# Attention values in a two-layer decoder trunk: unmasked weights on the left chunk's v, masked weights on the difference of both chunks' v, 512 columns a matmul

## The chip, the cores and the metric

The kernel runs on one core of one Trainium2 chip. The metric is the device time of one execution in microseconds (us). Before the change it is 2219.04 us, the median of three runs (2216.8 to 2220.34). The engines are called TensorE (PE, and PEld for its weight loads), VectorE (DVE), ScalarE (ACT), GpSimd (POOL) and SyncE (SP).

## The reference, cut to what matters

Input x is 2048 tokens by 1024 features, in float32. A first layer (a gated MLP with a spatial mix inside chunks of 128 tokens) is followed by a second: attention in a sliding window of 128 tokens, with 16 query heads of 64 features, 2 key/value heads, and a sink per head in the softmax. A query of chunk n sees keys of its own chunk and of the chunk to its left:

```python
k_band, v_band = band(k), band(v)          # chunk to the left, own chunk
rel = kj - CHUNK - qi
in_window = (rel <= 0) & (rel > -WINDOW)   # exactly 128 keys for each query
scores = where(mask, q . k_band * HEAD_DIM ** -0.5, -inf)
m = maximum(max(scores), sink)
p = exp(scores - m)
p = p / (sum(p) + exp(sink - m))
o = einsum('bnhrqk,bnkhd->bnqhrd', p, v_band)
y = o * silu(g)
return y @ w_out
```

For query i of a chunk, key j of the own chunk counts where j <= i, and key j of the left chunk where j > i. So each of the 128 places j belongs to exactly one of the two chunks, and one row of 128 weights holds them all. The trunk ends with a residual sum and a norm.

## The kernel before, in words

A float32 operand is split in two parts, high and low (`split`, L117 to L119: ACT casts the high part, DVE subtracts it from the operand). A product is then three matmuls (`mm3`, L121 to L124). The first layer (stage A) takes the first 1412 us and isn't touched. The second layer (stage B) goes through four blocks of 512 tokens, some 196 us each from the second on. A block has 18 pieces (`PIECES`): two for k and v (`kv_piece`, L879), eight for q, eight for the gate, and then the output projection (`outproj_b`, L1038). A counter of half pieces (`half`) sets off the attention steps among these matmuls: 16 tiles a block, one for four query heads and one chunk of 128 tokens, started at the counts in `ATT`. The steps of one tile are these:

- `scores` (L948): eight matmuls into two banks of PSUM (L966, L967), DVE merges the two chunks' scores into one row of 128 (L973) and takes the maximum (L974 to L982), ACT takes the exponentials (L984), and POOL divides by the sum (L991). A bank is free when ACT has read it.
- `turn_p` (L994), four half pieces later: four transposes on PE (L997), the high part on ACT (L999), the low part on DVE (L1000), then four selects on POOL (L1005): high and low with the own chunk's triangle kept, and high and low with the left chunk's triangle kept.
- `values` (L1011), three half pieces later: eight matmuls of 256 columns (L1019). The weights are v's high and low part, side by side (128 columns), so that the product has the high part's sum in one half of the partitions and the low part's in the other. The order is changed for the odd heads (low, high), for which `vst` holds the high part twice. ACT copies one half to the other's partitions (L1024, L1025), and DVE adds (L1026, L1027).

When the four tiles of a quad (four heads) are done, `gated` (L1029) multiplies by the gate (L1032) and splits for the output projection. The last quad's result is used by the fourth weight tile of the output projection, of which the first three run meanwhile. At about that time `hn_steps` (L310) also prepares the next block's input on DVE (L323, L119) and ACT (L118). POOL's queue also issues the loads of the projection weights (L190), each of which waits until PE has let go of the buffer. All short-lived tiles of stage B come from one pool of 39 slots of 512 columns (`GEN_B`). A scheduler places the instructions on each engine's queue, which is then worked off in order.

The diff touches `kv_piece`, `turn_p`, `values` and the tiles made ahead of them.

Of the kernel before, what the change touches and what calls it, by code (L numbers as in the profile page):

```python
# [12 lines left out]
F32 = mybir.dt.float32  # L13
F32R = mybir.dt.float32r
I32 = mybir.dt.int32
AF = mybir.ActivationFunctionType
ALU = mybir.AluOpType

P = 128
# [9 lines left out]
HD = 64  # L29
RING = 6  # L30
# [6 lines left out]
W_BUFS = 4  # L37
LOOKAHEAD = 3
GEN_A = 18
GEN_B = 39  # L40
RAW_A = 12
ST0 = 1
FIRST_W = (0, 2, 5)
# [19 lines left out]
def trunk(ctx: ExitStack, tc: tile.TileContext, xT, wv, wug, wao, wkv, wqg, wbo, wsT, bs, gains, lngb,  # L63
          bq, bkv, sinks, rot, masks, out):
    nc = tc.nc
    V, A, G, PE = nc.vector, nc.scalar, nc.gpsimd, nc.tensor
# [24 lines left out]
    def slot(dt=F32):  # L91
        return gen[0].tile([P, TB], dt, name="s", tag="s")

    def bank():
        return psum.tile([P, 512], F32, name="ps", tag="ps")
# [46 lines left out]
    def after(n, fn):  # L142
        at(now[0] + n, fn)
# [696 lines left out]
    bc = ctx.enter_context(tc.tile_pool(name="bc", bufs=1))  # L840
# [8 lines left out]
    sink_sb = bc.tile([P, 16], F32, name="sink_sb")  # L849
    nc.sync.dma_start(sink_sb, sinks.partition_broadcast(P))  # L850
    kst = bc.tile([P, 2, 2, RING, P], F32R, name="kst")
    vst = bc.tile([P, RING, 2, 3, HD], F32R, name="vst")
    V.memset(kst[:, :, :, RING - 1, :].bitcast(F32), 0.0)
    V.memset(vst[:, RING - 1].bitcast(F32), 0.0)

    def rope(src, nh, t0, nt, tab):
# [22 lines left out]
    def kv_piece(b, tp, w2, hh, hl, tab):  # L879
        if not w2:  # L880
            w2.extend([weights(), weights()])
        ps = bank()
        for t2 in range(2):
            natural(ps, t2, 2 * tp + t2, w2, hh, hl)
        kvs = slot()
        kv3 = kvs.rearrange("p (t n) -> p t n", t=2)
        V.tensor_tensor(kv3, ps.rearrange("p (t n) -> p t n", t=2), bkv_sb[:, None, :].broadcast_to([P, 2, 256]),
                        ALU.add)
        c0 = b * TT + 2 * tp
        kr = rope(kv3[:, :, 0:P].rearrange("p t (h d) -> p t h d", h=2), 2, 2 * tp, 2, tab)  # L890
        kr = kr.rearrange("p (t h d) -> p t h d", t=2, h=2)
        kss = []
        for t2 in range(2):
            sl = (c0 + t2) % RING
            ks = slot(F32R).rearrange("p (h s r d) -> p h s r d", h=2, s=2, r=2)
            src = kr[:, t2, :, None, :].broadcast_to([P, 2, 2, HD])
            A.copy(ks[:, :, 0], src)
            V.tensor_tensor(ks[:, :, 1], src, ks[:, :, 0].bitcast(F32), ALU.subtract)
            kss.append(ks)
            vsrc = kv3[:, t2, P:2 * P].rearrange("p (h d) -> p h d", h=2)  # L900
            A.copy(vst[:, sl, :, 0, :], vsrc)
            A.copy(vst[:, sl, :, 2, :], vsrc)
            V.tensor_tensor(vst[:, sl, :, 1, :], vsrc, vst[:, sl, :, 0, :].bitcast(F32), ALU.subtract)

        def turn():
            for t2 in range(2):
                sl = (c0 + t2) % RING
                pst = bank().bitcast(F32R)
                for i in range(4):
                    PE.transpose(pst[:, i * P:(i + 1) * P], kss[t2][:, i // 2, i % 2].rearrange("p r d -> p (r d)"),  # L910
                                 ident_r)
                A.copy(kst[:, :, :, sl, :], pst.bitcast(F32).rearrange("p (h s k) -> p h s k", h=2, s=2))

        after(K_T, turn)
# [79 lines left out]
    def turn_p(pn):  # L994
        ps = bank()
        for i in range(4):
            PE.transpose(ps[:, i * P:(i + 1) * P], pn[:, i * P:(i + 1) * P], ident)  # L997
        h_, l_ = slot(), slot()
        A.activation(h_.bitcast(F32R), ps, AF.Copy)  # L999
        V.tensor_tensor(l_, ps, h_, ALU.subtract)  # L1000
        pT = []
        for sign, base in ((1, 0), (-1, -1)):
            for x in (h_, l_):
                y = slot(F32R)
                G.affine_select(out=y.rearrange("p (h q) -> p h q", h=4), in_=x.rearrange("p (h q) -> p h q", h=4),  # L1005
                                pattern=[[0, 4], [sign, P]], base=base, channel_multiplier=-sign,
                                compare_op=ALU.is_ge, fill=0.0)
                pT.append(y)
        return [pT[:2], pT[2:]]

    def values(q, t, pT, halves, o):  # L1011
        kv = q // 2
        po = bank()
        for par in range(2):
            n = 0
            for ck in range(2):
                w = vst[:, halves[ck], kv, par:par + 2, :].rearrange("p r d -> p (r d)")
                for x in pT[ck]:
                    PE.matmul(po[:, par * 256:(par + 1) * 256], w, x[:, par * 256:(par + 1) * 256],  # L1019
                              start=n == 0, stop=n == 3)  # L1020
                    n += 1
        ov = o[:, :, t * P:(t + 1) * P]
        pe, pod = (po[:, i * 256:(i + 1) * 256].rearrange("p (i q) -> p i q", i=2) for i in range(2))
        A.copy(ov[0:64], pe[64:128])  # L1024
        A.copy(ov[64:128], pod[0:64])  # L1025
        V.tensor_tensor(ov[0:64], pe[0:64], ov[0:64], ALU.add)  # L1026
        V.tensor_tensor(ov[64:128], pod[64:128], ov[64:128], ALU.add)  # L1027
# [228 lines left out]
```

## Time and profile before

| what | value |
|---|---|
| median of three runs | 2219.04 us |
| profiled execution | 2223.57 us |
| its span | 2221.8 us |
| TensorE clock granted in it | 0.983 |
| PE busy | 2133.6 us, 96% |
| DVE busy | 1687.7 us, 76% |
| ACT busy | 1089.2 us, 49% |
| POOL busy | 1065.4 us, 48% |
| L1005, the selects on POOL | 256, 185.3 us |

The times of the profile count from the start of the span. Matmuls are pipelined: a row's duration for one matmul is its latency, and the pace is the step from one start to the next. In a row of the timeline stand the start, the duration, the engine, the line, the operation, the tiles written and read, the shapes and the count, and in brackets the idle time of the engine before it and what ended that.

### The profile page before, as it was taken

Reading aid. Unit: us, or ns where it says so; the run is one execution under the profiler, and the core shown is the slowest. Engines: PE = TensorE matmul, PEld = TensorE weight load, DVE = VectorE, ACT = ScalarE, POOL = GpSimd, SP = SyncE. Lnnn points to the kernel's source line nnn. Section 1 sums busy time; section 2 is a strip of 40 time slices with the busy share of each in tenths; the row PEclk is TensorE's granted clock in tenths of the full one; section 3 lists DMA queues with packets and bytes.
Section 4 is the critical chain, followed back from the end, with each engine's and each line's share of the span. In section 5 each row is a group of like instructions: output and inputs, shape, how many; then the busy total and the mean of one; then the engine's idle time right before and its main releaser. Section 6 shows DMA issues by size and latency. Waiting matters only on the chain.

```text
span 2221.8 us, 33592 instructions
## 1 busy us (share of the span) xinstructions
PE 2133.6 (96%) x11196; PEld 1809.7 (81%) x11196; DVE 1687.7 (76%) x2693; ACT 1089.2 (49%) x2431; POOL 1065.4 (48%) x1178
## 2 busy tenths in 40 slices
PE   7799999999899999999999899999999999999997
PEld 5578888888688777788888688898899889889986
DVE  9976778888986865766657987578867967986785
ACT  5225654445444534545444543257535834663573
POOL 3781446767544566644544445334415613451460
PEclk8899999999999999999999999999999999999999
DMA  8997555667786799634435796542463354346322
GB/s 290 318 348 243 169 183 182 197 209 242 265 297 224 265 326 330 211 117 147 154 110 157 250 324 206 197 141 102 140 225 114 127 195 163 114 128 243 115 96 95
DMA packets 208940, 441.95 MB, mean 199 GB/s; under 512 B 22656, under 2 KB 61824, under 8 KB 199552
## 3 DMA queue, kind: packets, MB, share of 16 engines
q1 hardware_dynamic: 163488, 255.76, 35.6%
q0 software_dynamic: 40672, 175.66, 21.7%
q10 hardware_dynamic: 4608, 8.39, 1.0%
q8 instruction: 89, 1.46, 0.3%
q14 instruction: 83, 0.68, 0.1%
HBM read 322.81 MB, written 116.92 MB: 198 GB/s over the span
## 4 chain that ended last, share of the span: by engine, by line
PE 45%; DVE 8%; issue 3%; ACT 2%; DMA 2%; POOL 1%; SPq 0%; DVEq 0%; POOLq 0%; ACTq 0%
PE ps L122 7%; PE ps L124 6%; PE ps L123 6%; PE ps L130 6%; PE ps L129 6%; PE ps L128 6%; PE ps L1019 2%; PE ps L997 1%; PE ps L635 1%; PE ps L966 1%; PE ps L967 1%; PE ps L938 1%; DVE hn L119 1%; DVE o L1027 1%; DVE wa L119 1%
## 5 line engine op out<-in xcount | busy, mean ns | idle before, releaser
L119 DVE TENSOR_TENSOR wa<-w_raw,wa 128x512 fp32r<-128x512 f32 x456 | 465.2, 1029 | 156.4 <-ACT wa L118 153.2
L130 PE MATMUL ps<-xh,wa 128*128 128x512 f32 x1344 | 529.5, 394 | 17.7 <-DVE wa L119 17.7
L128 PE MATMUL ps<-xh,wa 128*128 128x512 f32 x1344 | 530.9, 395 | 1.3 <-ACT s L549 1.0
L129 PE MATMUL ps<-xl,wa 128*128 128x512 f32 x1344 | 527.9, 393 | 0.0
L118 ACT CAST wa<-w_raw 128x512 fp32r<-128x512 f32 x456 | 280.5, 618 | 405.8 <-PE ps L130 303.7
L130 PEld LDWEIGHTS ps<-xh,wa 128*128 128x128 f32 x1344 | 253.2, 188 | 78.7 <-DVE wa L119 22.4
L128 PEld LDWEIGHTS ps<-xh,wa 128*128 128x128 f32 x1344 | 253.5, 189 | 57.1 <-ACT s L549 1.4
L129 PEld LDWEIGHTS ps<-xl,wa 128*128 128x128 f32 x1344 | 253.4, 189 | 55.6
L1005 POOL TENSOR_SCALAR_AFFINE_SELECT s<-s 128x512 fp32r<-128x512 f32 x256 | 185.3, 752 | 101.8 <-ACT s L999 69.5
L122 PE MATMUL ps<-w,hn 128*128 128x256 f32 x640 | 184.2, 288 | 0.0
L223 POOL TENSOR_TENSOR w_raw<-w_raw 128x512 f32<-128x512 f32 x48 | 75.0, 1565 | 226.0 <-DMA w_raw<-in_wug 134.3
L123 PE MATMUL ps<-w,hn 128*128 128x256 f32 x640 | 182.3, 285 | 0.0
L124 PE MATMUL ps<-w,hn 128*128 128x256 f32 x640 | 182.2, 285 | 0.0
L119 DVE TENSOR_TENSOR xl<-s,xh 128x512 fp32r<-128x512 f32 x168 | 137.4, 853 | 15.0 <-ACT xh L118 14.5
L190 POOL DMA_DIRECT2D w<-wb x72 | 40.6, 565 | 208.3 <-PE ps L124 182.6
L631 ACT ACTIVATE vp<-vp,nb,rs 128x128 f32<-128x128 f32 x256 | 106.7, 485 | 56.6 <-DMA vp<-v 47.8
L991 POOL TENSOR_TENSOR s<-s,rd 128x512 f32<-128x512 f32 x64 | 69.6, 1090 | 115.1 <-ACT s L999 47.0
L123 PEld LDWEIGHTS ps<-w,hn 128*128 128x128 f32 x640 | 124.0, 194 | 0.5
L122 PEld LDWEIGHTS ps<-w,hn 128*128 128x128 f32 x640 | 124.0, 194 | 0.5
L124 PEld LDWEIGHTS ps<-w,hn 128*128 128x128 f32 x640 | 123.9, 194 | 0.0
L123 PE MATMUL ps<-wa,xh 128*128 128x512 f32 x256 | 104.7, 409 | 19.0 <-DVE wa L119 18.9
L225 POOL TENSOR_TENSOR w_raw<-w_raw 128x512 f32<-128x512 f32 x48 | 66.3, 1386 | 103.2 <-DVE wa L119 102.2
(190 smaller groups left out, 5011.4 us busy)
## 6 DMA issues: line engine op xcount, KB each, us to landing
w<-wb POOLq DMA_DIRECT2D x72, 1024.0 KB, 5.3
w_raw<-in_wug SPq DMA_DIRECT2D x160, 256.0 KB, 3.3
w_raw<-in_wv SPq DMA_DIRECT2D x88, 256.0 KB, 5.4
s<-in_xT SPq DMA_DIRECT2D x80, 256.0 KB, 4.8
w_raw<-in_wao SPq DMA_DIRECT2D x80, 256.0 KB, 4.1
wb<-s POOLq DMA_DIRECT2D x72, 256.0 KB, 5.8
vp<-v SPq DMA_DIRECT2D x32, 512.0 KB, 4.6
Y_s<-s POOLq DMA_DIRECT2D x64, 256.0 KB, 3.9
```

The source lines that it names most:

```text
L118: A.copy(hi, src)
L119: (lo_eng or V).tensor_tensor(lo, src, hi.bitcast(F32), ALU.subtract)
L122: PE.matmul(ps, ah, bh, start=first, stop=False)
L123: PE.matmul(ps, ah, bl, start=False, stop=False)
L124: PE.matmul(ps, al, bh, start=False, stop=last)
L128: PE.matmul(ps, ah, bh, start=first, stop=False, skip_group_check=True)
L129: PE.matmul(ps, ah, bl, start=False, stop=False, skip_group_check=True)
L130: PE.matmul(ps, al, bh, start=False, stop=True, skip_group_check=True)
L223: G.tensor_tensor(u["22"], u["21"], u["22"], ALU.add)
L631: A.activation(v[:, c, :], v[:, c, :], AF.Identity, bias=nb[:, c:c + 1], scale=rs[:, c:c + 1])
L991: G.tensor_tensor(p4, p4, rd[:, :, None].broadcast_to([P, 4, P]), ALU.mult)
L1005: G.affine_select(out=y.rearrange("p (h q) -> p h q", h=4), in_=x.rearrange("p (h q) -> p h q", h=4), pattern=[[0, 4], [sign, P]], base=ba ...
```

## The change

For each query the weights stand in one row of 128. Where `pm` is the row with only the own chunk's triangle kept, the sum over both chunks is p times the left chunk's v plus `pm` times (own v minus left v). The new kernel computes this. `kv_piece` forms the difference of each chunk's v and its left neighbour's (`vd`; the last chunk of a piece is kept in `vl` for the next) and splits it into `vdt`. `turn_p` masks the high and the low part once, not twice. `values` does four matmuls of 512 columns, two with the unmasked parts and two with the masked ones. The pool of slots has 38 and not 39.

```diff
-GEN_B = 39
+GEN_B = 38
...
-    vst = bc.tile([P, RING, 2, 3, HD], F32R, name="vst")
+    vst = bc.tile([P, RING, 2, 2, HD], F32R, name="vst")
+    vdt = bc.tile([P, RING, 2, 2, HD], F32R, name="vdt")
+    vl = bc.tile([P, P], F32, name="vl")
+    V.memset(vl, 0.0)
...
+        vd = slot()[:, :256].rearrange("p (t n) -> p t n", t=2)
+        V.tensor_tensor(vd[:, 0], kv3[:, 0, P:2 * P], vl, ALU.subtract)
+        V.tensor_tensor(vd[:, 1], kv3[:, 1, P:2 * P], kv3[:, 0, P:2 * P], ALU.subtract)
+        A.copy(vl, kv3[:, 1, P:2 * P])
...
             A.copy(vst[:, sl, :, 0, :], vsrc)
-            A.copy(vst[:, sl, :, 2, :], vsrc)
             V.tensor_tensor(vst[:, sl, :, 1, :], vsrc, vst[:, sl, :, 0, :].bitcast(F32), ALU.subtract)
+            dsrc = vd[:, t2].rearrange("p (h d) -> p h d", h=2)
+            A.copy(vdt[:, sl, :, 0, :], dsrc)
+            V.tensor_tensor(vdt[:, sl, :, 1, :], dsrc, vdt[:, sl, :, 0, :].bitcast(F32), ALU.subtract)
...
-        for sign, base in ((1, 0), (-1, -1)):
-            for x in (h_, l_):
-                y = slot(F32R)
-                G.affine_select(out=y.rearrange("p (h q) -> p h q", h=4), in_=x.rearrange("p (h q) -> p h q", h=4),
-                                pattern=[[0, 4], [sign, P]], base=base, channel_multiplier=-sign,
-                                compare_op=ALU.is_ge, fill=0.0)
-                pT.append(y)
+        pT = [h_, l_]
+        for x in (h_, l_):
+            y = slot(F32R)
+            G.affine_select(out=y.rearrange("p (h q) -> p h q", h=4),
+                            in_=x.bitcast(F32).rearrange("p (h q) -> p h q", h=4), pattern=[[0, 4], [1, P]], base=0,
+                            channel_multiplier=-1, compare_op=ALU.is_ge, fill=0.0)
+            pT.append(y)
...
-        for par in range(2):
-            n = 0
-            for ck in range(2):
-                w = vst[:, halves[ck], kv, par:par + 2, :].rearrange("p r d -> p (r d)")
-                for x in pT[ck]:
-                    PE.matmul(po[:, par * 256:(par + 1) * 256], w, x[:, par * 256:(par + 1) * 256],
-                              start=n == 0, stop=n == 3)
-                    n += 1
+        n = 0
+        for v, pair in ((vst[:, prv, kv], pT[0]), (vdt[:, cur, kv], pT[1])):
+            w = v.rearrange("p r d -> p (r d)")
+            for x in pair:
+                PE.matmul(po, w, x, start=n == 0, stop=n == 3)
+                n += 1
```

The scheduler orders the instructions anew. Lines from L854 on have other numbers in the changed kernel (L1005 is L1013, L991 is L1000, L1019 is L1029, L984 is L993, L986 is L995, L1024 and L1025 are L1033 and L1034). Three places follow, of the kernel before and then of the changed one.

On DVE, at the start of stage B, where the first piece of k and v is taken in (L887), rotated (L863 to L867), and split for k (L898) and v (L903). Before:

```order
L887 TENSOR_TENSOR s<-ps,bkv_sb 128x512
L903 TENSOR_TENSOR vst<-s,vst 128x2x64
L863 TENSOR_TENSOR s<-s 128x256
L864 TENSOR_TENSOR s<-s 128x256
L903 TENSOR_TENSOR vst<-s,vst 128x2x64
L866 TENSOR_TENSOR s<-s 128x4x32
L867 TENSOR_TENSOR s<-s 128x4x32
L255 TENSOR_TENSOR s<-ps,ident 128x512
L898 TENSOR_TENSOR s<-s 128x2x128 x2
```

The same place in the changed kernel, where L896 and L897 are the two differences and L912 is the low part of `vdt`:

```order
L890 TENSOR_TENSOR s<-ps,bkv_sb 128x512
L909 TENSOR_TENSOR vst<-s,vst 128x2x64 x2
L866 TENSOR_TENSOR s<-s 128x256
L867 TENSOR_TENSOR s<-s 128x256
L896 TENSOR_TENSOR s<-s,vl 128x128
L869 TENSOR_TENSOR s<-s 128x4x32
L870 TENSOR_TENSOR s<-s 128x4x32
L897 TENSOR_TENSOR s<-s 128x128
L912 TENSOR_TENSOR vdt<-s,vdt 128x2x64
L255 TENSOR_TENSOR s<-ps,ident 128x512
L905 TENSOR_TENSOR s<-s 128x2x128 x2
L912 TENSOR_TENSOR vdt<-s,vdt 128x2x64
```

Three of the four added instructions now stand ahead of the split of k (L898, now L905), and one behind it.

On POOL, some 85 us into the second block, where w is the buffer of the projection weights. Before:

```order
L190 DMA w<-wb_224 128x2048
L1005 AFFINE_SELECT s<-s 128x512 x4
L190 DMA w<-wb_225 128x2048
L991 TENSOR_TENSOR s<-s,rd 128x512 x2
L1005 AFFINE_SELECT s<-s 128x512 x2
L991 TENSOR_TENSOR s<-s,rd 128x512
```

In the changed kernel:

```order
L190 DMA w<-wb_224 128x2048
L1013 AFFINE_SELECT s<-s 128x512 x2
L1000 TENSOR_TENSOR s<-s,rd 128x512
L190 DMA w<-wb_225 128x2048
L1000 TENSOR_TENSOR s<-s,rd 128x512 x2
L1013 AFFINE_SELECT s<-s 128x512 x2
```

One division by the sum (L991, now L1000) has moved from behind the weight load to ahead of it.

On ACT, at the same time, where the copies of a tile's values and the exponentials of two later tiles meet. Before:

```order
L986 ACTIVATE es<-es 128x4
L1024 COPY o<-ps 64x2x128
L1025 COPY o<-ps 64x2x128
L984 ACTIVATE s,den<-ps,nm 128x128 x8
L986 ACTIVATE es<-es 128x4
L946 COPY sg<-ps 128x512
```

In the changed kernel:

```order
L995 ACTIVATE es<-es 128x4
L993 ACTIVATE s,den<-ps,nm 128x128 x8
L995 ACTIVATE es<-es 128x4
L1033 COPY o<-ps 64x2x128
L1034 COPY o<-ps 64x2x128
L955 COPY sg<-ps 128x512
```

The two copies have moved behind the eight exponentials.

More of the change, by code (lines that the diff above doesn't have):

```diff
@@ L997, in turn_p @@
             PE.transpose(ps[:, i * P:(i + 1) * P], pn[:, i * P:(i + 1) * P], ident)
[L998 to L1001, printed above, removed]
-        for sign, base in ((1, 0), (-1, -1)):
-            for x in (h_, l_):
-                y = slot(F32R)
-                G.affine_select(out=y.rearrange("p (h q) -> p h q", h=4), in_=x.rearrange("p (h q) -> p h q", h=4),
-                                pattern=[[0, 4], [sign, P]], base=base, channel_multiplier=-sign,
-                                compare_op=ALU.is_ge, fill=0.0)
-                pT.append(y)
+        h_, l_ = slot(F32R), slot(F32R)
+        A.activation(h_, ps, AF.Copy)
+        V.tensor_tensor(l_, ps, h_.bitcast(F32), ALU.subtract)
+        pT = [h_, l_]
[5 more added lines that the diff above has]
+            pT.append(y)
         return [pT[:2], pT[2:]]
@@ L1012, in values @@
         kv = q // 2
+        cur, prv = halves
         po = bank()
-        for par in range(2):
-            n = 0
-            for ck in range(2):
-                w = vst[:, halves[ck], kv, par:par + 2, :].rearrange("p r d -> p (r d)")
-                for x in pT[ck]:
-                    PE.matmul(po[:, par * 256:(par + 1) * 256], w, x[:, par * 256:(par + 1) * 256],
-                              start=n == 0, stop=n == 3)
-                    n += 1
+        n = 0
[4 more added lines that the diff above has]
+                n += 1
         ov = o[:, :, t * P:(t + 1) * P]
```

## The prediction

> **What bounds the kernel now.** I read the page first: busy time by engine, then the forty slices.
>
> ```profile
> PE 2133.6 (96%) x11196; PEld 1809.7 (81%) x11196; DVE 1687.7 (76%) x2693; ACT 1089.2 (49%) x2431; POOL 1065.4 (48%) x1178
> PE   7799999999899999999999899999999999999997
> DVE  9976778888986865766657987578867967986785
> ```
>
> PE sets the time in nearly every slice. The change touches only stage B, about the last 15 slices, so what it can win there is PE work that goes away and PE waits that go away. The table of windows shows where the waits are: start of stage B, end of its first block, and most of the second block.
>
> ```profile
> 1412.00:1455.00 43.00, 36.20 (x253) 34.26 (x252) 20.05 (x48) 8.25 (x22) 10.06 (x12) 0.90 0.52 184
> 1562.00:1600.00 38.00, 36.17 (x188) 29.93 (x187) 36.16 (x54) 22.95 (x53) 21.14 (x23) 1.00 0.48 153
> 1600.00:1680.00 80.00, 80.00 (x552) 73.82 (x551) 49.68 (x114) 28.24 (x81) 14.48 (x21) 1.00 0.61 211
> ```
>
> After the window's bounds and length come the busy times of PE, PEld, DVE, ACT and POOL. Between 1600 and 1680 PE never rests. At the first block's end it rests 1.8 us, and there DVE is as busy as PE (36.2 of 38 us). At the start it rests 6.8 us. The groups by line name what ended these rests, after the second bar.
>
> ```profile
> L122 PE MATMUL ps<-s,w 128*128 128x512 f32 x224 | 88.2, 399 | 3.9 <-ACT s L118 3.8
> L938 PE MATMUL ps<-ident_r,s 128*128 128x128 f32 x256 | 28.6, 249 | 5.7 <-ACT s L984 3.7 <-DVE s L931 2.0
> L910 PE MATMUL ps<-ident_r,s 128*128 128x128 f32 x64 | 7.2, 254 | 4.8 <-ACT s L897 4.7
> ```
>
> The last of the output projection's weight tiles waits 3.8 us in all for the last quad's gated values (L118). The transposes of q wait 3.7 us for exponentials that free a bank of PSUM. The start of stage B waits 4.7 and 2.0 us. The values matmuls wait for POOL, by the view of that line:
>
> ```profile
> L1019 PE MATMUL ps<-s,vst x512: 276/281/388, 1486.0 to 2177.7; 128*128 128x256 f32 x171
>   POOL s L1005: 2.4, 9
> ```
>
> The waits that the change can reach are these 2.4, 3.8 and 3.7 us, about 10 us of 2222.
>
> **The change, term by term.** 1. PE work. Both forms stream 2048 columns a tile: eight matmuls of 256, or four of 512. Two undisturbed groups give their pace.
>
> ```profile
> 1583.58 1.08 PE L1019 MATMUL ps<-s,vst 128*128 128x256 f32 x8
> 1584.50 0.39 PE L122 MATMUL ps<-s,w 128*128 128x512 f32 x1
> ...
> 1590.06 1.32 PE L1019 MATMUL ps<-s,vst 128*128 128x256 f32 x8
> ```
>
> ```profile
> 1695.74 1.11 PE L1019 MATMUL ps<-s,vst 128*128 128x256 f32 x8
> 1696.69 0.46 PE L938 MATMUL ps<-ident_r,s 128*128 128x128 f32 x4
> ```
>
> Eight narrow ones take 0.92 us from start to next start in the first group and 0.95 in the second. Between 1584.50 and 1590.06 stand 24 wide ones: 5.56/24 = 0.232 us each, four take 0.927. So a tile gains between -0.007 and 0.023 us, and 64 tiles between -0.4 and 1.5 us. I take 0.5 us gained. That the matmuls are halved in number is worth next to nothing.
>
> [...]
>
> 2. The selects. 128 of the 256 leave POOL, and the first two values matmuls no longer read a select's output. Their parts, `h_` and `l_`, come from ACT and DVE ahead of the selects. The third one needs the first select, where it used to need the third. I take all of the 2.4 us away, with 1.6 as the lower end: nine waits stand in the row, and some would return if PE came sooner.
>
> 3. The ends of the blocks. This is the end of the first one: the values of the last tile, what ACT and DVE do with them, and PE's wait.
>
> ```profile
> 1587.29 3.19 POOL L1005 TENSOR_SCALAR_AFFINE_SELECT s<-s 128x512 fp32r<-128x512 f32 x3 [3.12 <-DVE s L1000]
> 1588.27 1.12 DVE L119 TENSOR_TENSOR hn<-s,hn 128x512 fp32r<-128x512 f32 x1
> 1592.92 0.68 DVE L119 TENSOR_TENSOR hn<-s,hn 128x512 fp32r<-128x512 f32 x1
> 1593.77 0.37 ACT L1024 COPY o<-ps 64x256 f32<-64x256 f32 x1
> 1596.25 1.22 DVE L1032 TENSOR_TENSOR o<-o,sg 128x1024 f32<-128x1024 f32 x1
> 1598.23 0.97 PE L122 MATMUL ps<-s,w 128*128 128x512 f32 x3 [1.28 <-ACT s L118]
> ```
>
> The values were done by 1591.4, but ACT copies them at 1593.77, since its queue first casts what DVE hands it, and DVE is behind. And DVE is behind partly because of POOL: the same subtraction takes 1.12 us beside a select and 0.68 when POOL is idle. Over the last 34 us of the block the groups of DVE show it:
>
> ```profile
> L119 DVE TENSOR_TENSOR hn<-s,hn 128x512 fp32r<-128x512 f32 x8 | 6.8, 856 | 0.1
> L323 DVE TENSOR_TENSOR s<-s 128x512 f32<-128x512 f32 x8 | 6.7, 862 | 0.1
> L119 DVE TENSOR_TENSOR s<-o,s 128x512 fp32r<-128x512 f32 x2 | 2.1, 1056 | 0.0
> L987 DVE TENSOR_TENSOR den<-den,es 128x4 f32<-128x4 f32 x2 | 1.2, 610 | 0.0
> ```
>
> Against 0.68 us the first three lose 8 x 0.176 + 8 x 0.182 + 2 x 0.376 = 3.6 us. With the half of the selects half of that goes, 1.8 us (an estimate); the small operations, such as L987 with 0.61 us for four columns, come on top. The wait is 1.28 us, and PE itself arrives earlier by its part of term 2 (2.4 us over four blocks, 0.6 each): 1.9 us are needed, and about as much is there. So I take the whole 3.8 us; the lower end is nothing, if the order of POOL's selects and DVE's work falls badly. The orders of DVE and ACT over this stretch stay nearly as they were.
>
> 4. The waits for exponentials. The timeline of the second block shows one that comes back in the third and fourth:
>
> ```profile
> 1701.23 0.55 POOL L190 DMA_DIRECT2D w<-wb  x1 [3.67 <-PE ps L124]
> 1701.80 2.05 POOL L991 TENSOR_TENSOR s<-s,rd 128x512 f32<-128x512 f32 x2
> 1701.86 2.28 DVE L866 TENSOR_TENSOR s<-s 128x256 f32<-128x256 f32 x1
> ...
> 1707.93 0.53 PE L938 MATMUL ps<-ident_r,s 128*128 128x128 f32 x4 [0.56 <-ACT s L984]
> ```
>
> POOL's weight load waits for PE, two divisions pile up behind it, and DVE's rotation (L866), which runs beside them, takes 2.28 us. What hangs on it on ACT, casts and then exponentials, comes late. In the new order one division stands ahead of the load, so it should be over before L866 starts: DVE gains about one division, 1.0 us, which is more than 0.56. I take 3 x 0.56 = 1.7 us. The upper end is all of the 3.7 us, the lower end nothing.
>
> 5. The start of stage B. DVE gets four more instructions for each of the eight `kv_piece`, ACT one more. In the later blocks they fall into the stretch in which PE never rests and DVE is busy 49.7 of 80 us: 0. In the first block DVE is late, and PE waits for it.
>
> ```profile
> 1447.82 0.28 DVE L866 TENSOR_TENSOR s<-s 128x128 f32<-128x128 f32 x1
> 1448.02 0.28 DVE L867 TENSOR_TENSOR s<-s 128x128 f32<-128x128 f32 x1
> ...
> 1452.54 0.76 DVE L931 TENSOR_TENSOR s<-s 128x256 fp32r<-128x256 f32 x2 [0.17 <-ACT s L930]
> 1453.03 1.11 PE L938 MATMUL ps<-ident_r,s 128*128 128x128 f32 x8 [1.96 <-DVE s L931]
> 1454.00:1460.00 6.00, 6.00 (x43) 6.00 (x42) 2.41 (x6) 2.66 (x6) 1.09 (x2) 0.77 0.47 178
> ```
>
> An instruction of this size takes 0.20 us from start to start. Two pieces come ahead of the first transposes of q, so 8 x 0.20 = 1.6 us are lost, with nothing to hide them: the queue behind them (L923, L931) is what PE waits for. The lower end is 0.8, if only the second piece's count. The granted clock was 0.77 in the 6 us after this wait. Were the wait twice as long and as much clock lost again, 6 x 0.23 = 1.4 us would come on top, so the upper end is 3.0.
>
> The sum: 0.5 + 2.4 + 3.8 + 1.7 - 1.6 = 6.8 us gained. The profiled execution took 2223.57 us (span 2221.8, and 1.8 around it), so it would take 2216.8. The median of the runs is 4.5 us below the profiled one, and from 2219.04 the same 6.8 us give 2212.2. By the ends of the terms the gain lies between 1.6 - 3.0 - 0.4 = -1.8 and 1.5 + 2.4 + 3.8 + 3.7 - 0.8 = 10.6 us, 2208.4 to 2220.8. All ends don't fall on one side, and for the forecast alone I take a gain of 3 to 11 us, 2208 to 2216.
>
> **The rivals.** First: the waits only move. Terms 3 and 4 don't come, because DVE stays as far behind at the end of a block, with what PE gains ahead of it waited away there; of term 2 a third is left. That gives 0.5 + 0.8 - 1.6 = -0.3 us, 2219.3. For it speaks that DVE is busy 36.2 of 38 us there, with PE waiting for its results; against it, that DVE itself loses time to the very selects that go.
>
> [...]
>
> Third, the other side: banks of PSUM. At the place shown on ACT, the copies that free the values' bank have moved behind eight exponentials. Their group gives the price:
>
> ```profile
> L984 ACT ACTIVATE s<-ps,nm 128x128 f32<-128x128 f32 x256 | 90.8, 375 | 26.9 <-DVE es L982 25.6 <-DVE nm L980 1.0
> ```
>
> Eight of them take 8 x 90.8/256 = 2.8 us, and the bank is held so much longer, once a block. If PE's next matmuls need just this bank, it waits for up to that long four times, 11.2 us, and the time is 2219.0 - 6.8 + 11.2 = 2223.4. It decides from a wait of 1.7 us a block, at which the gain is gone; the result is slower by over 4.4 us only near its whole price. For it speaks that PE waits for a bank in this very place (part of the 3.7 us); against it, that the exponentials free four other banks meanwhile, and come sooner without the copies ahead of them.
>
> That the change doesn't do what it says is no rival of its own: term 1 has that already.
>
> **How the numbers follow.** A measurement of this kernel can tell about 0.2%, 4.4 us, from no change. The forecast has a chance of 0.68, the first rival 0.18, the second 0.02, the third 0.12. Of the forecast's own cases (gains of 3 to 11 us) I put a tenth below 4.4 us, since two of the large terms would have to fail for that: 0.61 faster, 0.07 the same. The first rival is the same. Of the third, 0.08 are slower, and 0.04 the same. With the second that is 0.63 faster, 0.29 the same, 0.08 slower. The predicted time is 2212.2. The range runs from 2207.0, a little below the forecast's own low end (DVE may gain elsewhere too), to 2219.5, which takes in the first rival; the second and most of the third stay outside.
>
> **What would show it.** In the profile after: the values' step for four wide matmuls near 0.93 us (term 1); no wait for POOL at their line (2); the output projection's wait for L118 near zero in all blocks, with the mean of DVE's 128x512 subtractions at a block's end near 0.77 us (3); the second block's rotation near 1.2 us and the wait of 0.56 gone (4); the first transposes of q waiting some 3.5 us instead of 1.96 (5). [...]

## The result, and the profile after

The changed kernel takes 2205.94 us, the median of four runs (2205.36 to 2209.21), against 2219.69 us for the kernel before on the same chip (2216.8 to 2220.45). The ratio is 0.9943, with a 95% interval from 0.9926 to 0.9961: faster by 0.4 to 0.7%. The forecast was 2212.2 us, faster. The sign and most places are right, but the time lies 1.1 us below the low end of the range, and the 13.7 us gained are twice the forecast's 6.8. In the two profiles 10.7 us of the gain lie in stage B, which the change touches.

The profiled execution took 2205.87 us, its span 2204.0. The page after, busy time by engine:

```profile
PE 2130.6 (97%) x10940; PEld 1798.8 (82%) x10940; DVE 1657.0 (75%) x2726; ACT 1093.0 (50%) x2439; POOL 973.6 (44%) x1050
```

DVE has 33 instructions more than before and is busy 30.7 us less, 28.4 us of that in the four blocks. Where the time went shows in the table of windows, cut at the first scores matmul of each block: first the start of stage B (from the last matmul of stage A), then the four blocks. Before:

```profile
1432.74:1458.95 26.21, 19.41 (x110) 17.65 (x109) 18.32 (x46) 9.14 (x25) 4.86 (x7) 0.80 0.40 143
1458.95:1655.08 196.13, 192.85 (x1264) 173.38 (x1262) 152.71 (x340) 105.36 (x294) 76.07 (x100) 1.00 0.42 144
1655.08:1850.79 195.71, 193.36 (x1270) 174.06 (x1269) 151.59 (x332) 105.29 (x294) 75.95 (x99) 1.00 0.45 154
1850.79:2046.52 195.73, 193.45 (x1271) 174.13 (x1269) 151.39 (x332) 105.31 (x294) 76.96 (x101) 1.00 0.45 154
...
2046.55:2221.80 175.25, 162.10 (x1106) 147.06 (x1104) 126.12 (x301) 99.45 (x279) 67.48 (x91) 0.97 0.32 109
```

And after:

```profile
1425.68:1452.16 26.48, 19.47 (x103) 17.54 (x102) 19.99 (x54) 9.64 (x27) 4.86 (x7) 0.81 0.36 129
1452.16:1646.52 194.36, 192.18 (x1207) 170.99 (x1206) 146.18 (x348) 106.11 (x296) 52.74 (x68) 1.00 0.43 146
1646.52:1838.67 192.15, 192.00 (x1206) 170.63 (x1205) 143.84 (x341) 106.07 (x296) 52.51 (x67) 1.00 0.45 157
1838.67:2030.80 192.13, 191.97 (x1206) 170.62 (x1205) 143.89 (x341) 106.06 (x296) 53.58 (x69) 1.00 0.46 157
...
2030.80:2204.00 173.20, 161.35 (x1042) 143.69 (x1040) 119.49 (x302) 99.48 (x279) 45.23 (x59) 0.97 0.33 111
```

The first number behind the bounds is the length, the third busy time is DVE's, the fifth POOL's. The blocks are shorter by 1.8, 3.6, 3.6 and 2.1 us, and in each DVE is busy 6.5 to 7.8 us less and POOL 22 to 23 us less. All of stage B takes 778.3 us, and 789.0 before: 10.7 us. The rest of the 17.8 us between the two spans is stage A, counted to its last matmul, which the change doesn't touch. It took 1432.7 us in the profile of before and 1425.7 in that of after, and between 1425.2 and 1431.7 in the twelve later runs, whichever kernel it was. Stage B of the changed kernel came out at 778.3 and 778.7 us in two profiles; the kernel before was profiled once. So small effects are read from stage B, not from the whole time.

PE's waits in stage B, by line:

```profile
L122 PE MATMUL ps<-s,w 128*128 128x512 f32 x224 | 88.1, 399 | 0.6
L975 PE MATMUL ps<-kst,s 128*128 128x256 f32 x256 | 63.2, 281 | 1.1 <-ACT s L949 1.1
L1029 PE MATMUL ps<-s,vst 128*128 128x512 f32 x128 | 42.6, 414 | 0.0
L947 PE MATMUL ps<-ident_r,s 128*128 128x128 f32 x256 | 27.4, 245 | 2.3 <-DVE s L940 2.3
L919 PE MATMUL ps<-ident_r,s 128*128 128x128 f32 x64 | 7.4, 254 | 4.7 <-ACT s L904 4.4 <-DVE s L905 0.3
L122 PE MATMUL ps<-hn,w 128*128 128x512 f32 x256 | 102.7, 401 | 0.9 <-PE ps L976 0.9
```

The 3.9 us at the output projection are 0.6, the 3.7 us for exponentials are gone, and the values wait for nothing. At the start 4.8 and 2.0 us have become 4.7 and 2.3. Two waits of the first block are new: 1.1 us ahead of scores and 0.9 us ahead of a gate matmul.

The end of the first block, in the timeline after:

```profile
1582.86 0.63 PE L1029 MATMUL ps<-s,vst 128*128 128x512 f32 x2
1583.33 0.63 PE L1029 MATMUL ps<-s,vdt 128*128 128x512 f32 x2
1583.79 0.39 PE L122 MATMUL ps<-s,w 128*128 128x512 f32 x1
...
1584.65 0.37 ACT L1033 COPY o<-ps 64x256 f32<-64x256 f32 x1
...
1586.99 1.23 DVE L1041 TENSOR_TENSOR o<-o,sg 128x1024 f32<-128x1024 f32 x1
...
1588.97 0.96 PE L122 MATMUL ps<-s,w 128*128 128x512 f32 x3
```

The four values matmuls take 0.93 us. ACT copies them 0.7 us after their end (2.4 us before), the gate's product starts 3.0 us after it (4.9 before), and PE finds its operand nearly ready.

### The profile page after: what moved, and what is told of

Same layout as the page of the kernel before. It is cut to its first block, busy times and chain, and to the rows that moved or that the text cites. A ratio compares the mean times of both kernels' runs of the same rounds, so it can differ in the third digit from the quotient of the medians.

```text
span 2204.0 us, 32953 instructions
## 1 busy us (share of the span) xinstructions
PE 2130.6 (97%) x10940; PEld 1798.8 (82%) x10940; DVE 1657.0 (75%) x2726; ACT 1093.0 (50%) x2439; POOL 973.6 (44%) x1050
## 4 chain that ended last, share of the span: by engine, by line
PE 78%; DVE 8%; DMA 5%; issue 3%; POOL 2%; ACT 2%; SPq 1%; DVEq 0%; POOLq 0%; ACTq 0%
PE ps L130 12%; PE ps L128 12%; PE ps L129 12%; PE ps L122 11%; PE ps L123 10%; PE ps L124 10%; PE ps L1029 3%; PE ps L635 2%; DVE wa L119 2%; PE ps L975 1%; PE ps L976 1%; PE ps L1006 1%; PE ps L947 1%; DVE xl L119 1%; DMA s<-Y_s 1%
## 5 line engine op out<-in xcount | busy, mean ns | idle before, releaser
L130 PEld LDWEIGHTS ps<-xh,wa 128*128 128x128 f32 x1344 | 253.8, 189 | 74.9 <-DVE wa L119 18.3
L223 POOL TENSOR_TENSOR w_raw<-w_raw 128x512 f32<-128x512 f32 x48 | 78.6, 1639 | 222.6 <-DMA w_raw<-in_wug 136.8
L1000 POOL TENSOR_TENSOR s<-s,rd 128x512 f32<-128x512 f32 x64 | 72.2, 1129 | 183.0 <-ACT s L1008 75.3
L1013 POOL TENSOR_SCALAR_AFFINE_SELECT s<-s 128x512 fp32r<-128x512 f32 x128 | 89.5, 714 | 106.2 <-ACT s L1008 83.8
L118 ACT CAST xh<-s 128x512 fp32r<-128x512 f32 x168 | 97.6, 617 | 34.8 <-DMA s<-X_s 9.6
```

The source lines that it names most:

```text
L118: A.copy(hi, src)
L130: PE.matmul(ps, al, bh, start=False, stop=True, skip_group_check=True)
L223: G.tensor_tensor(u["22"], u["21"], u["22"], ALU.add)
L1000: G.tensor_tensor(p4, p4, rd[:, :, None].broadcast_to([P, 4, P]), ALU.mult)
```

## The experiments

Stage times of all profiled runs in us, read from the starts of the same matmuls as above. "Start" is the start of stage B, the last block runs to the end of the span, the last two columns are the median of all runs and the ratio on record to the kernel before on the same chip, which is not quite the quotient of the medians.

| kernel | start | block 1 | 2 | 3 | 4 | stage B | median | ratio (95%) |
|---|---|---|---|---|---|---|---|---|
| before | 26.2 | 196.1 | 195.7 | 195.7 | 175.3 | 789.0 | | |
| changed | 26.5 | 194.4 | 192.2 | 192.1 | 173.2 | 778.3 | 2205.94 | 0.9943 (0.9926 to 0.9961) |
| changed, again | 26.7 | 194.4 | 192.2 | 192.1 | 173.2 | 778.7 | 2208.33 | 0.9940 (0.9922 to 0.9957) |
| 1 wide matmuls only | 24.5 | 199.0 | 195.4 | 195.4 | 175.2 | 789.5 | 2217.77 | 0.9994 (0.9985 to 1.0003) |
| 2 narrow matmuls | 27.3 | 194.6 | 197.1 | 198.3 | 173.1 | 790.3 | 2219.43 | 1.0008 (0.9996 to 1.0021) |
| 3 two unread selects | 28.1 | 198.1 | 195.3 | 195.5 | 175.4 | 792.3 | 2222.64 | 1.0014 (1.0004 to 1.0024) |
| 4 no difference | 26.4 | 193.6 | 192.1 | 192.3 | 173.2 | 777.6 | 2206.93 | 0.9950 (0.9931 to 0.9968) |
| 5 difference later | 25.8 | 192.6 | 192.2 | 192.2 | 173.2 | 775.9 | 2205.95 | 0.9944 (0.9926 to 0.9962) |
| 6 narrow, three raw buffers | 26.1 | 196.3 | 196.0 | 197.5 | 173.1 | 789.1 | 2217.32 | 0.9995 (0.9986 to 1.0005) |
| 7 POOL work alone | 33.7 | 212.6 | 192.1 | 192.1 | 172.8 | 803.4 | 2234.55 | 1.0072 (1.0052 to 1.0092) |
| 8 selects twice | 27.6 | 200.9 | 199.5 | 198.1 | 176.5 | 802.6 | 2232.14 | 1.0068 (1.0048 to 1.0088) |
| 9 narrow, input later | 27.0 | 196.3 | 195.3 | 195.2 | 173.2 | 787.0 | 2215.41 | 0.9983 (0.9972 to 0.9994) |
| 10 changed, input later | 27.8 | 195.4 | 193.2 | 193.1 | 173.3 | 782.8 | 2212.91 | 0.9977 (0.9966 to 0.9989) |
| 11 before, input later | 25.5 | 195.2 | 195.2 | 195.1 | 174.3 | 785.2 | 2216.84 | 0.9989 (0.9977 to 1.0002) |

The theory at the outset was the prediction's: two selects less a tile free POOL and DVE, and PE's waits go. The rivals were the width of the matmuls, and later the order in which the scheduler puts the queues, since every edit makes it draw up a new one.

**The changed kernel again.**

> The changed kernel once more, as it is. In the two profiles so far, stage A (up to the last matmul ahead of the first k transposes) ended 7.1 us earlier in the changed kernel, although the change does not touch it, and from the first scores matmul to the end it took 751.8 us where the kernel before took 762.9. Theory: the 7.1 us of stage A vary from run to run, the 11 us of stage B do not. So stage B again takes 751.8 within 0.5 us, and stage A differs by some us from either. Rival: something of the change reaches into stage A; then stage A ends at about 1425.7 us again, here and in every kernel with the changed code.

It gave 0.9940, and stage B within 0.4 us of the first time: the result stands. By the medians (2208.33 against 2218.05 us) it gained 9.7 us here and 13.7 us the first time.

**1. Wide matmuls only.** The kernel before, with four matmuls of 512 columns but all four selects.

```diff
-        for par in range(2):
-            n = 0
-            for ck in range(2):
-                w = vst[:, halves[ck], kv, par:par + 2, :].rearrange("p r d -> p (r d)")
...
+        n = 0
+        for ck in range(2):
+            w = vst[:, halves[ck], kv, 0:2, :].rearrange("p r d -> p (r d)")
...
+                PE.matmul(po, w, x, start=n == 0, stop=n == 3)
```

> The kernel before, with four values matmuls of 512 columns in place of eight of 256; four selects on POOL as before, no difference of v. Theory (the selects on POOL pay): the width alone gives 0 to 1.5 us, so stage B from the first scores matmul takes 761.5 to 763, and the waits at the blocks' ends (1.28 us) stay. Rival (fewer matmuls pay): most of the 11 us, 752 to 755.

**2. Narrow matmuls.** The changed kernel, with eight matmuls of 256 columns and two selects.

```diff
+        for par in range(2):
+            n = 0
+            for v, pair in ((vst[:, prv, kv], pT[0]), (vdt[:, cur, kv], pT[1])):
...
+                    PE.matmul(po[:, par * 256:(par + 1) * 256], w, x[:, par * 256:(par + 1) * 256],
```

> The changed kernel with its two masked and two unmasked parts, but with eight values matmuls of 256 columns. Theory (the selects pay): stage B from the first scores matmul takes 752 to 754 us, nearly all of the gain. Rival (fewer matmuls pay): 759 to 763.

The two leave no gain each, which as whole times reads as if both halves of the change were needed. The last block, in which no input of a next block is prepared, says otherwise. Wide matmuls with four selects:

```profile
2040.55:2215.70 175.15, 161.84 (x1042) 143.85 (x1040) 125.02 (x301) 99.56 (x279) 67.43 (x91) 0.98 0.33 110
```

Narrow matmuls with two selects:

```profile
2044.50:2217.60 173.10, 161.27 (x1106) 146.85 (x1104) 118.59 (x302) 99.61 (x279) 46.11 (x59) 0.97 0.33 112
```

With the 175.25 and 173.20 us of before and after this is a full square: in this block the width is worth 0.1 us or nothing, the selects 2.0 us, and DVE is busy 5.5 to 7.5 us less where POOL does two selects, not four. The 2.0 us aren't free of the order: the kernel before takes 174.3 us here in experiment 11. But the nine profiles in which POOL does two selects a tile in this block all lie between 172.8 and 173.3 us, and the five with four between 174.3 and 176.5. What the narrow kernel loses, it loses at the ends of the blocks and in a slow clock behind them (last section). Its line of the output projection, and then the end of its second block, on SP's queue and on DVE's:

```profile
L122 PE MATMUL ps<-s,w 128*128 128x512 f32 x224 | 89.6, 406 | 9.8 <-ACT s L118 9.6
```

```profile
1764.78 0.33 SPq L89 DMA_DIRECT2D w_raw<-in_wbo  x1
1765.21 0.85 SPq L322 DMA_DIRECT2D s<-h  x2
1767.21 0.33 SPq L89 DMA_DIRECT2D w_raw<-in_wbo  x1
1767.64 2.47 SPq L322 DMA_DIRECT2D s<-h  x5
```

```profile
1770.12 0.69 DVE L323 TENSOR_TENSOR s<-s 128x512 f32<-128x512 f32 x1 [2.22 <-DMA s<-h]
```

DVE stands still for 2.22 us, waiting for the next block's input `h`. SP issues its last five loads only at 1767.64, behind a load of raw weights that waits for a buffer; in the changed kernel's queue that load stands two loads of `h` later. PE then waits 3.6 us for the gated values (3.9 in the third block). That was the cause to test next.

**3. Two unread selects.** The changed kernel, with two more selects a tile that nothing reads.

```diff
+        for x in (h_, l_):
+            y = slot(F32R)
+            G.affine_select(out=y.rearrange("p (h q) -> p h q", h=4),
```

> The changed kernel, with two more selects on POOL behind the two that are used, of the same size, whose results nobody reads. So the values no longer wait for them, but POOL and DVE share the work as before. Theory (DVE is slowed by the selects, and so late at the blocks' ends): 4 to 8 of the 11 us are lost again, stage B takes 756 to 760, with a wait of over 0.8 us at the end of a block. Rival (only the values' own wait for the select pays, and the new order): stage B stays at 752 to 753.5.

The gain is gone, 2.2 us of it in the last block (175.4 us). But SP's queue had the narrow kernel's order here, and so had that of experiment 1. What they lose at the ends of the blocks can't be put down to selects or width alone. (The kernel before has the changed kernel's order on SP, so the gain between these two isn't SP's.)

**4. No difference.** The changed kernel without forming v's difference (the masked weights use the own chunk's v, so the output is not the reference's).

```diff
-        V.tensor_tensor(vd[:, 0], kv3[:, 0, P:2 * P], vl, ALU.subtract)
-        V.tensor_tensor(vd[:, 1], kv3[:, 1, P:2 * P], kv3[:, 0, P:2 * P], ALU.subtract)
-        A.copy(vl, kv3[:, 1, P:2 * P])
...
-        for v, pair in ((vst[:, prv, kv], pT[0]), (vdt[:, cur, kv], pT[1])):
+        for v, pair in ((vst[:, prv, kv], pT[0]), (vst[:, cur, kv], pT[1])):
```

> The changed kernel without the difference of the two chunks' v: the masked weights use the own chunk's v as it is, so the output is not the reference's. PE's matmuls and POOL's selects are those of the changed kernel and nearly all instructions stand in its order; 32 instructions of DVE and 8 of ACT are gone. Theory of the prediction (DVE's queue at the start of stage B sets PE's waits there): from the last matmul of stage A to the first scores of the first block 26.5 becomes 25.0 to 25.5 us, the four blocks stay as they are within 0.3 us each, the whole is 1.0 to 1.6 us below the changed kernel. Rival (the added instructions are covered after all): stage B 778.3 us as in the changed kernel, within 0.3.

Stage B is 0.8 us shorter, 0.1 in the start and 0.7 in the first block, where the expectation had 1.0 to 1.5 us in the start and nothing in the blocks. Only 0.2 us of it are shorter waits of PE, the rest is the clock (term 5 below). So the added instructions cost 0.2 to 0.8 us, half of the term's 1.6 us at most.

**5. Difference later.** The changed kernel, with the difference and its split in the later step that transposes k (the lines move from `kv_piece` into its `turn`).

> The changed kernel, with the difference of v and its split formed in the later step that transposes k, behind what the first transposes of q wait for, and not in the step that takes in k and v. Theory of the prediction: the start of stage B is 1.0 to 1.6 us shorter (26.5 to about 25 us) and nothing else moves, stage B about 777 us against 778.3. Rival (what is moved only makes the next step on DVE or ACT late): start as before, or the first block longer by as much, stage B 778 us or more. The first values matmuls of a block come over 30 us later, so none of them should wait for the moved instructions.

Stage B is 2.5 us shorter, but not as expected. The waits at the start are nearly those of the changed kernel (4.1 and 2.2 us, there 4.4 and 2.3); what went is most of the slow stretches behind them. The 4 us behind the second wait, in the changed kernel:

```profile
1447.00:1451.00 4.00, 3.99 (x24) 3.99 (x25) 3.02 (x7) 1.67 (x5) 0.00 (x0) 0.60 0.47 184
```

and in this one:

```profile
1447.77:1451.77 4.00, 4.00 (x35) 4.00 (x36) 3.49 (x10) 0.97 (x4) 0.00 (x0) 1.00 0.53 211
```

The column behind POOL's is the granted clock, 0.60 against 1.00. PE worked at half clock for 10.0 us at the start of the changed kernel's stage B, and for 3.4 us here; half of the difference, 3.3 us (an estimate), more than covers the gain. This is luck: as the last section shows, the clock was set in cells of 3.41 us, and here the second wait lies across a border between two of them (PE rests 1.65 us in the first, 0.58 in the next), while the changed kernel's lies in one (2.28). By stage B this is the fastest version, but its 2205.95 us can't be told from the changed kernel's 2205.94.

**6. Narrow, three raw buffers.** `W_RAW_BUFS` 3, `GEN_B` 36, on experiment 2.

> The changed kernel with eight matmuls of 256 columns, as in the run before with narrow matmuls, but with three buffers for raw weights and not two (36 slots and not 38). The orders of PE, DVE, ACT and POOL are those of that run. There the last loads of h for the next block stood behind a load of raw weights on SP's queue, which waited for a buffer until DVE had split the weights before, and PE then waited 2.1, 3.6 and 3.9 us at the ends of the first three blocks. Theory that this place in SP's queue cost the gain, not the width: these three waits fall below 1 us each, the blocks come within 1 us of the changed kernel's (192 to 193 us for the second and third), the whole about 2209 to 2212 us. Rival (narrow matmuls themselves, or DVE's order, cost it): the waits stay above 2 us, the whole 2217 to 2220 us.

The waits stayed, 2.2, 2.6 and 4.1 us, but the run doesn't decide: with one more buffer SP's queue loads one weight further ahead, and the load in the same place waits for the same split as before (issued at 1765.96, when that split had ended). The wait on SP was not taken away.

**7. POOL work alone.** The changed kernel, with two more selects a tile that read the bias of q and write a tile of their own, and 37 slots, not 38.

```diff
+        for _ in range(2):
+            G.affine_select(out=jk.rearrange("p (h q) -> p h q", h=4),
+                            in_=bq_sb[:, :TB].rearrange("p (h q) -> p h q", h=4), pattern=[[0, 4], [1, P]], base=0,
```

> The changed kernel with two more selects a tile on POOL, which read the bias of q and write a tile of their own, so that nothing waits for them and no slot is held for them; 37 slots and not 38. SP's order is that of the changed kernel, PE's differs in one stretch of the first block. Theory that POOL's work by itself slows DVE and delays POOL's queue: DVE's subtractions of 128x512 that stand beside them lengthen from 0.69 towards 1.1 us, PE's waits at the ends of blocks come back with about 1 us each, and those for exponentials in the second to fourth block with 0.5 to 0.9 us; stage B loses 4 to 8 of its 11 us. Rival (the gain came from the order in which the scheduler put the other queues, or from the values no longer needing four selects): stage B loses under 2 us.

Since they depend on nothing, POOL ran all 128 by 1580 us. First and second block:

```profile
1461.12:1673.80 212.68, 197.79 (x1205) 172.38 (x1206) 164.53 (x348) 106.91 (x297) 126.26 (x171) 0.98 0.38 134
1673.80:1865.90 192.10, 191.96 (x1207) 170.64 (x1206) 143.57 (x341) 105.96 (x296) 52.40 (x67) 1.00 0.45 157
```

Start and first block are 7.2 and 18.3 us longer than the changed kernel's, the second as short as there. So 128 selects that no other engine waits for, 93 us on POOL, cost 25 us, far over the 4 to 8 expected. They came bunched, not two a tile, and the waits expected at the ends of the blocks stayed at 0.13 us. POOL's work by itself is paid for by PE: DVE is 18.4 us busier for the same instructions in the first block, values and exponentials wait behind POOL's queue, and PE rests 14.9 us there (2.2 in the changed kernel).

**8. Selects twice.** The changed kernel, each of its two selects done a second time into the same slot.

```diff
+        for x, y in zip((h_, l_), pT[2:]):
+            G.affine_select(out=y.rearrange("p (h q) -> p h q", h=4),
```

> The changed kernel with its two selects of a tile done twice, the second time into the same slots, so that POOL has four selects a tile as before, no slot is held more, and the result is the same; the masked matmuls wait for the second time. SP's order is that of the changed kernel; PE's, DVE's and ACT's differ from it in single stretches. Theory that the two selects less are the gain (POOL's work slows DVE and holds up POOL's queue): PE's waits at the ends of blocks come back with 1 to 2 us each, those for exponentials with 0.5 to 0.9 us in the second to fourth block, stage B takes 784 to 789 us against 778.3. Rival (the gain came from the order in which the scheduler put the other queues): stage B under 780.5 us.

```profile
L122 PE MATMUL ps<-s,w 128*128 128x512 f32 x224 | 89.4, 405 | 7.8 <-ACT s L118 7.6
...
L947 PE MATMUL ps<-ident_r,s 128*128 128x128 f32 x256 | 28.3, 248 | 6.8 <-ACT s L993 3.9 <-DVE s L940 2.8
```

At the changed kernel's SP order, the waits of the kernel before come back, those at the ends of blocks with 2.5 us each, and the last block takes 176.5 us. It loses 24 us, over twice the change's gain; why four selects cost more here than in the kernel before stays open.

**9, 10, 11. Input later.** The narrow kernel, the changed one and the one before, each with `HN0 = 36` and not 35, so that the next block's input is prepared one half piece later. SP's order is then the same in all three.

> The changed kernel with eight matmuls of 256 columns, and with the next block's input prepared one half piece later (HN0 is 36 and not 35). PE's and POOL's orders are those of the run with narrow matmuls, ACT's nearly; SP's puts five loads of h, not three, between the load of raw weights in their midst and the next two, as in the changed kernel with 36, which is timed beside it. Theory that the place of the weight load in SP's queue cost the narrow kernel the gain: PE's waits at the ends of the blocks fall from 2.1, 3.6 and 3.9 us to under 1 us each, and stage B comes within 2 us of the changed kernel's with 36. Rival (narrow matmuls, or the order of DVE that comes with them, cost it): the waits stay above 2 us, stage B 787 to 791 us.

> The changed kernel with the next block's input prepared one half piece later (HN0 is 36 and not 35), as the control for the two other runs with 36. PE's and POOL's orders are those of the changed kernel. Theory: DVE has enough left at the ends of the blocks, their waits stay below 0.5 us, and stage B takes 778 to 780 us. Rival (the changed kernel's ends of blocks are only just met): waits of over 1 us come back there, stage B 781 us or more.

> The kernel before with the next block's input prepared one half piece later (HN0 is 36 and not 35). SP's order is the same as in the changed kernel with 36. Theory that four selects a tile, with POOL's and DVE's queues, make the waits of the kernel before: stage B 788 to 792 us, 9 to 12 us more than the changed kernel's with 36, with waits of 1 to 3 us at the ends of the blocks. Rival (the gain of the change hung on the one order that it happened to get): the difference between the two kernels with 36 is under 5 us.

All three expectations fell. The narrow kernel's waits stay at 2.2, 1.8 and 3.3 us, so the place of the weight load in SP's queue doesn't explain them alone. The changed kernel's waits come back, 1.15 us in each of three blocks, no shorter than the 1.05 us of the kernel before with 36. Changed kernel with 36:

```profile
L122 PE MATMUL ps<-s,w 128*128 128x512 f32 x224 | 88.1, 399 | 3.6 <-ACT s L118 3.4
...
L947 PE MATMUL ps<-ident_r,s 128*128 128x128 f32 x256 | 27.8, 247 | 3.0 <-DVE s L940 3.0
```

Kernel before with 36:

```profile
L122 PE MATMUL ps<-s,w 128*128 128x512 f32 x224 | 88.2, 399 | 3.3 <-ACT s L118 3.1
...
L938 PE MATMUL ps<-ident_r,s 128*128 128x128 f32 x256 | 28.6, 249 | 5.5 <-ACT s L984 3.5 <-DVE s L931 1.9
```

Between these two kernels lie 2.4 us in stage B, not 10.7: under 5 us, as the rival had it by which the gain hung on one order. From the first scores on it is 4.7 us, not 11.0, and 3.9 us lie between their medians. The waits for exponentials go with the selects here too (3.5 us, then none); the waits at the ends of the blocks don't. And the start of the changed one is 2.3 us longer, with waits of 4.7 and 3.0 us against 4.1 and 1.9, and one slow stretch of the clock more.

## Why the prediction was right or wrong

From the first scores to the last matmul the changed kernel's PE takes 10.7 us less. By what PE had just started, counting from each start to the next: values 65.6 to 61.9 us, transposes of q 23.9 to 20.0, transposes of p 24.8 to 23.3, matmuls of 512 columns (with most of the waits at the ends of blocks) 340.6 to 335.9. Those of 256 columns went from 234.9 to 236.9 and scores from 60.8 to 61.9, with the two new waits in them; transposes of k are unchanged.

**Terms 1 and 2, values** (0.5 and 2.4 us): right, though not all of the 3.7 us is theirs. By the steps inside the tiles the waits for POOL took 3.0 us and the width gives 0.1; the other 0.7 us was a wait for exponentials right behind a values matmul. (The row with 2.4 us counts waits of the weight loads too.) The width is 0.1 us a block or nothing (experiments 1 and 2, last block), four wide matmuls step by 0.93 us, and the wait for POOL is gone. The second rival (chance 0.02), a better pace for wide matmuls, is out by the same row; no run shows one, and the 0.93 us stand in its place.

**Term 3, ends of the blocks** (3.8 us): the row went from 3.9 to 0.6 us, so the size is right. DVE's work there became cheaper as forecast. Its groups over the last 34 us of the first block:

```profile
L119 DVE TENSOR_TENSOR hn<-s,hn 128x512 fp32r<-128x512 f32 x8 | 6.7, 842 | 0.1
L323 DVE TENSOR_TENSOR s<-s 128x512 f32<-128x512 f32 x8 | 5.3, 681 | 0.1
L119 DVE TENSOR_TENSOR s<-o,s 128x512 fp32r<-128x512 f32 x3 | 2.1, 686 | 1.0 <-ACT s L118 1.0
```

Their mean is 0.75 us (0.77 forecast, 0.88 before), though the first group hardly changed (856 to 842 ns). But the reason was only half of it. With two selects a tile this wait was 0.14 us (the changed kernel, experiments 4, 5 and 7, whose added selects were over by then), 1.15 (10) and 1.8 to 4.1 (2, 6, 9), with four 1.05 to 2.5 (before, 1, 3, 8, 11). The term's lower end, "if the order of POOL's selects and DVE's work falls badly", is what experiments 2, 6, 9 and 10 met. That fewer selects alone remove this wait is refuted; which of the orders on DVE, ACT and SP decides it stays open.

**Term 4, exponentials** (1.7 us): mis-sized. The whole 3.7 us went, the upper end. The step that failed is the count: I took the three waits of 0.56 us whose chain I had followed, and left the rest. Of the kernels with two selects only experiment 5 has one of these waits (0.5 us in the first block) and experiment 7, with its added work, several; experiments 1, 3, 8 and 11, with four, have 3.4 to 3.9 us. So this wait goes with the selects in every order tried. The chain itself is as forecast, in the second block after:

```profile
1690.66 1.33 POOL L1000 TENSOR_TENSOR s<-s,rd 128x512 f32<-128x512 f32 x1 [3.53 <-DVE rd L998]
1692.17 0.60 POOL L190 DMA_DIRECT2D w<-wb  x1 [0.17 <-issue]
1692.35 0.39 DVE L869 TENSOR_TENSOR s<-s 128x256 f32<-128x256 f32 x1
```

One division stands ahead of the load, and the rotation that took 2.28 us takes 0.39. The 1.5 us of the transposes of p were not foreseen.

**Term 5, start of stage B** (-1.6 us): mis-sized, at most -0.8 by experiment 4, the term's lower end. DVE is later, as worked out, but the second wait grew only from 1.96 to 2.28 us, not to the forecast's 3.5, since PE itself comes to it 0.7 us later. In all the waits there are 7.0 us, 6.8 in experiment 4. The rest of the 0.8 us is the clock: half pace for 10.0 us, 8.9 in experiment 4. That loss stood only in the term's upper end, and it depends on where the clock's cells fall (last section), which the change doesn't set.

**Not in the sum:** the two new waits of the first block, 2.0 us against the change. They are about what that block gains less than the next two (1.8 against 3.6 us). The wait ahead of scores goes with the wide matmuls: eight of the nine profiles with them have 1.1 to 1.4 us some 50 us into the first block, and none of the five with narrow ones has it there. Why is not shown.

**First rival**, waits only move: out for this order. With `HN0` 36 half of it holds: the waits at the ends of the blocks stay (term 3), those for exponentials go (term 4). **Third rival**, the values' bank: no matmul in the middle of the second to fourth block waits for it.

Fewer selects didn't speed up every instruction of DVE. The subtraction that reads PSUM takes the same in the kernel before and the changed one, at the ends of the second blocks:

```profile
L1000 DVE TENSOR_TENSOR s<-ps,s 128x512 f32<-128x512 f32 x6 | 4.1, 686 | 1.2 <-ACT s L999 1.1
```

```profile
L1009 DVE TENSOR_TENSOR s<-ps,s 128x512 fp32r<-128x512 f32 x3 | 2.1, 692 | 0.1
```

The product of two slots (L323) went from 862 to 681 ns. Over all of stage B of the kernel before, the 64 of L1000 take 652 to 694 ns, wherever POOL's selects stand, and the 24 of L323 take 659 to 1123. Of these, the six that lie beside selects from start to end take 1.11 to 1.12 us, and the nine with POOL idle 0.68 to 0.69. In the changed kernel no L323 takes more than 694 ns, not even the three that lie wholly beside a select. What makes this difference is not shown.

## What to carry to other kernels

Work on an engine that nobody seems to wait for can still be on the bill: 128 selects that nothing read cost 25 us here, bunched as they came, so price such work by what it does to its neighbour's instructions. Compare edits stage by stage, and where there is one, in a stage that has only what the edit touches: the last block told width from selects, 0.1 from 2.0 us, where the whole times misled. And where a scheduler orders the queues anew after each edit, try the edit at a second order before its gain is put down to it: here stage B gained 10.7 us at one and 2.4 at the other, of which the luck of the clock has its part too.

## What was not expected of the hardware

A wait of PE may cost more than its length. Behind the wait of 3.63 us at the end of the narrow kernel's second block, the next 4 us:

```profile
1787.30:1791.30 4.00, 4.00 (x13) 3.04 (x13) 1.92 (x3) 1.06 (x2) 0.00 (x0) 0.69 0.46 158
```

The clock was 0.69, and the whole block is 4.9 us longer than the changed kernel's. Experiment 9 shows what decides it. Its second block ends with a wait of 1.79 us, its third with one of 3.25 us:

```profile
1786.05:1789.46 3.41, 1.62 (x7) 1.03 (x6) 2.54 (x4) 1.14 (x2) 0.00 (x0) 1.00 0.74 272
1789.46:1792.88 3.42, 3.42 (x9) 2.58 (x9) 1.90 (x4) 0.62 (x1) 0.00 (x0) 0.50 0.29 113
...
1980.61:1984.02 3.41, 1.86 (x8) 1.15 (x7) 3.10 (x6) 1.62 (x4) 0.00 (x0) 1.00 0.18 34
1984.02:1987.43 3.41, 1.70 (x7) 1.26 (x8) 2.60 (x4) 1.14 (x2) 0.00 (x0) 1.00 0.91 351
1987.43:1990.84 3.41, 3.41 (x17) 2.75 (x16) 1.53 (x3) 1.25 (x2) 0.00 (x0) 1.00 0.00 0
```

The shorter wait is followed by a clock of 0.50, with matmuls of 512 columns at 0.43 us a step; the longer one is not. The bounds of these rows are no free choice. In each of the fourteen profiles the stretches at half clock begin whole multiples of 3.413 us apart and, the one at the very end aside, last a whole multiple of it. So in these profiles the clock is set in cells of 3.41 us. The 1.79 us lie in one cell, and PE is busy for 1.62 us of it; the 3.25 us lie across a border, and each cell keeps 1.86 and 1.70 us of work. I counted over stage B of all fourteen profiles, from its first slow stretch to 2190 us. All 20 cells at full clock in which PE rested 1.88 us or more were followed by a slow one, two of the four with 1.79 to 1.84, and of those with 1.70 us or less a single one (experiment 1, 1.22 us).

Where the borders fall differs from profile to profile: the first slow stretch of stage B begins 2.5 to 5.2 us after the last matmul of stage A. So each slow cell, up to 1.7 us of loss (half of its 3.41 us, an estimate), is partly luck. With half of PE's busy time at half clock taken off (an estimate), stage B takes 784.7 us before, 773.4 changed, 773.1 and 774.1 in experiments 4 and 5, 780.2 in experiment 2, and 777.2 and 781.1 in experiments 10 and 11. Experiment 5 has no lead then, the narrow kernel gains 4.5 us after all, and the two kernels with `HN0` 36 lie 3.9 us apart, as their medians do.
